# Gate and up product of a hybrid decoder block: where the second half's norm matmuls stand, and which engine does its last squares and low parts

## The chip, the cores and the metric

The kernel runs on one core of one Trainium2 chip. The metric is the device time of one execution in microseconds (us). Three runs of the kernel before gave 1517.66, 1513.57 and 1512.15 us; the median is 1513.57 us.

## What is computed

One decoder block over 1024 tokens of width 1024 in float32: two attention branches (sparse attention and a gated delta rule), an output projection with a residual, then a gated feed-forward network with an inner width of 2816, and a final norm. The change lies where the output projection ends and the feed-forward network begins:

```
x = x + jnp.concatenate([o_nsa, o_gdn], axis=-1) @ w_out
h = rmsnorm(x, norm2_g)
x = x + (jax.nn.silu(h @ w_gate) * (h @ w_up)) @ w_down

def rmsnorm(x, g):
    y = x * lax.rsqrt(jnp.mean(x * x, axis=-1, keepdims=True) + RMS_EPS)
    return y * g
```

## The kernel before

The kernel holds activations with the width on the 128 partitions and the tokens along the free axis, in two halves of 512 tokens (hf 0 and 1) and 8 slices of 128 of the width (dt 0 to 7). To keep float32 accuracy each matmul operand is split in a high part (a rounded copy, written by ScalarE) and a low part (the source less the high part, written by VectorE or GpSimd), and each product of two such pairs is three matmuls: `split3`, lines 116 to 121, high by high (L119), high by low (L120), low by high (L121).

**Output projection.** `woa(hf, dt)` multiplies for one slice; `woa_out(hf, dt)` (L1169 to L1176) adds the residual on VectorE (L1172), stores the result and passes it to `sumsq` (L1185): ScalarE squares it (L1187, tile wx), and for dt 1 to 5 GpSimd adds the square to the running sum sqa (L1191). The squares of dt 6 and 7 are not added: they go as two more tiles to the list parts[hf].

**Norm.** `rnorm_sum` (L1202) sums over partitions on TensorE: for each of four token blocks and each of the three tiles (sqa and the two of parts) a matmul with two columns of ones (L1208). The profile shows two records for each such float32 matmul, so 24. VectorE scales the sum (L1211), GpSimd takes the power of minus one half (L1212), and `rnorm_out` (L1215) spreads the result over the partitions with four matmuls (L1219, 8 records). `normed` (L1356, L1357) scales one slice on VectorE with the result straight from PSUM. `bsplit` (L1360) splits a scaled slice: high part on ScalarE (L1361), low part on the engine that is passed in (L1362).

**Gate and up.** The weights come in blocks b = 0 to 21 (gate and up alternate for 11 pairs of blocks). Every block but the first is made with a scheme of seven products in place of eight, on sums and differences of quarters: of the activations B11, B21 (first half of the tokens), B12, B22 (second half) and the sums T1 to T4, and of the weights A11, A12, A22 and the sums S1 to S4. `Weights.second` (L1335) loads the raw quarters (L1324, five raw buffers), forms the sums on VectorE (L1339 to L1342) and splits them (ScalarE L1199, GpSimd L1200). The sums of block 1 are split behind the power of the second half's norm on GpSimd (mark["pow"], L1343).

Block 0 is done plainly with `prod2` (L1382): 8 steps of k, 24 matmuls, into one bank. The order in the text is: c11 = prod2 with A11, A12 on the first half; `rnorm_sum` of the second half; c21 = prod2 with A21, A22; `rnorm_out`; then the products A11 by B11 and A12 by B21 of blocks 1 and 2 (L1398, 48 matmuls), which need only the first half. Then the second half is scaled and split: 8 times `normed` with `bsplit` on GpSimd (L1410 to L1415), then the differences for T1 to T4 and their splits on VectorE (L1416 to L1427: 16 differences and sums, 16 low parts). With B12 and B22 the two other plain products of block 0 follow (L1437, L1438, 48 matmuls), then for block 1 the products S2 by T2, S3 by T3, S1 by T1, A22 by T4 and S4 by B22, 60 matmuls.

**What sets the order.** Each engine runs its own instructions in order. A planner fixes that order: it takes the instructions in the order of the text, but an instruction that is not ready by its own estimate lets later ones of the same engine pass. `after(ins, prev)` adds an order without a semaphore: ins stands behind prev on their engine. The ring (L1195) is a set of 20 buffers of 128 by 512 that holds the 16 slices of the two halves, the four t2, and later the gate's results (`gated`, L1431), each of which takes the buffer of a slice that is no longer needed. The PSUM pool of this stage has 8 banks.

Of the kernel before, what the change touches and what calls it, by code (L numbers as in the profile page):

```python
# [10 lines left out]
F32 = mybir.dt.float32  # L11
# [8 lines left out]
P = 128  # L20
# [3 lines left out]
KD = D // P  # L24
# [55 lines left out]
def hybrid_block(ctx, tc, xT, xN, pos, cst_d, vec_d, w_tok, w_gdn, cw1, cw2, cpos, w_out, w_gu, w_dn, out):  # L80
# [7 lines left out]
    def mk(pool, shape, tag, dtype=F32, bufs=1):  # L88
        return pool.tile(list(shape), dtype, name=nm(tag), tag=tag, bufs=bufs)
# [10 lines left out]
    def bc(ap, shape):  # L100
        return ap.to_broadcast(list(shape))

    def flat(ap):
        return ap.rearrange("p h t -> p (h t)")
# [4 lines left out]
    mm = nc.tensor.matmul  # L109
# [3 lines left out]
    V = nc.vector  # L113
    G = nc.gpsimd

    def split3(ps, lhs, rhs, first, last, grow=False):

        (lh, ll), (rh, rl) = lhs, rhs
        mm(ps, lhsT=lh, rhs=rh, start=first, stop=False, skip_group_check=grow)  # L119
        mm(ps, lhsT=lh, rhs=rl, start=False, stop=False, skip_group_check=grow)  # L120
        return mm(ps, lhsT=ll, rhs=rh, start=False, stop=last, skip_group_check=grow)  # L121

    def after(ins, prev):

        if prev is not None:
            tc.add_manual_dep(ins.ins, prev.ins.name, mybir.DependencyInfo(
                mybir.DependencyClass.NoSync, mybir.DependencyReason.DATA), reason="order")
        return ins
# [45 lines left out]
    ident = C("ident")  # L174
# [994 lines left out]
    def woa_out(hf, dt):  # L1169
        ps, xt, _ = woas[hf, dt]  # L1170
        x2 = xs2[hf, dt] = ring()
        V.tensor_tensor(out=x2, in0=xt, in1=ps, op=ALU.add)  # L1172
        dma(x3D[hf, dt], x2)
        t = sumsq(sqa[hf], x2, dt, 512, G if dt < 6 else None, flat(mk(pmx, [P, 4, P], "wx", F32, 3)))
        if dt >= 6:
            parts[hf].append(t)  # L1176

    woas = {}
# [6 lines left out]
    def sumsq(sqa, x2, dt, w, eng, tmp):  # L1185
        s_ = tmp if dt else sqa
        act(out=s_[:, :w], in_=x2, func=AF.Square)  # L1187
        if eng is None:
            return tmp
        if dt:  # L1190
            eng.tensor_tensor(out=sqa[:, :w], in0=sqa[:, :w], in1=s_[:, :w], op=ALU.add)  # L1191

    mark = {}
# [8 lines left out]
    def rnorm_sum(parts, w, prev=None):  # L1202

        n = w // P
        ps = bank2("n")
        for j in range(n):
            for q_, t in enumerate(parts):
                after(mm(ps[:, 2 * j:2 * j + 2], lhsT=t[:, j * P:(j + 1) * P], rhs=ones[:, 0:2], start=q_ == 0,  # L1208
                         stop=q_ == len(parts) - 1), prev)
        ms = mk(pc, [P, 2, 4], "ms4", F32, 2)  # L1210
        V.tensor_scalar(ms[:, 0, 0:n], ps[:, 0:2 * n:2], 1.0 / D, EPS, op0=ALU.mult, op1=ALU.add)  # L1211
        mark["pow"] = G.tensor_tensor(out=ms[:, 1, 0:n], in0=ms[:, 0, 0:n], in1=C("mhalf")[:, 0:n], op=ALU.pow)  # L1212
        return ms

    def rnorm_out(ms, w, prev=None):  # L1215

        ps = bank2("n")
        for j in range(w // P):
            after(mm(ps[:, j * P:(j + 1) * P], lhsT=bc(ms[:, 1, j:j + 1], [P, P]), rhs=ident, start=True, stop=True),  # L1219
                  prev)  # L1220
        return ps[:, 0:w]

    merge((scores(us[0]), wa(0)))
# [46 lines left out]
    def bank2(tag="mm"):  # L1270
        return mk(pps2, [P, 512], "mm", F32, 8)
# [84 lines left out]
    def normed(hf, dt, rB):  # L1356
        V.scalar_tensor_tensor(out=xs2[hf, dt], in0=xs2[hf, dt], scalar=VC("g2")[:, dt:dt + 1], in1=rB,  # L1357
                               op0=ALU.mult, op1=ALU.mult)

    def bsplit(B, k, src, eng):  # L1360
        act(out=B[:, 0, k], in_=src, func=AF.Copy)  # L1361
        eng.tensor_tensor(out=B[:, 1, k], in0=src, in1=f32(B[:, 0, k]), op=ALU.subtract)  # L1362
# [16 lines left out]
            wts[b] = Weights(b // 2, b % 2)  # L1379
            wts[b].first() if b else wts[b].plain()  # L1380
    P12 = {}
    def prod2(A, B, A_, B_):  # L1382

        ps = bank2()
        for k in range(8):
            a_, b_ = (A, B) if k < 4 else (A_, B_)
            e = split3(ps, (a_[:, 0, k % 4], a_[:, 1, k % 4]), (b_[:, 0, k % 4], b_[:, 1, k % 4]), k == 0, k == 7)
            if k == 3:
                mid = e
        return ps, mid, e  # L1390


    W = wts.pop(0)
    c11, mid, _ = prod2(W.A11, B11, W.A12, B21)
    ms1_ = rnorm_sum([sqa[1]] + parts[1], 512, mid)
    c21, mid, _ = prod2(W.A21, B11, W.A22, B21)
    rB1 = rnorm_out(ms1_, 512, mid)
    for b in range(1, NAHEAD):  # L1398
        p1, e = prod(wts[b].A11, B11)
        p2, e = prod(wts[b].A12, B21)  # L1400
# [6 lines left out]
    h = [(xs2[0, k], xs2[0, 4 + k], xs2[1, k], xs2[1, 4 + k]) for k in range(4)]  # L1407
    t2 = {}
    B12 = mk(pms, [P, 2, 4, 512], "mns", F32R, 1)
    for k, (h0a, h0b, h1a, h1b) in enumerate(h):  # L1410
        normed(1, k, rB1)
        bsplit(B12, k, h1a, G)
    for k, (h0a, h0b, h1a, h1b) in enumerate(h):
        normed(1, 4 + k, rB1)
        bsplit(B22, k, h1b, G)  # L1415
    for k, (h0a, h0b, h1a, h1b) in enumerate(h):  # L1416
        V.tensor_tensor(out=h0a, in0=h1a, in1=h0a, op=ALU.subtract)
        t2[k] = ring()
# [12 lines left out]
    def gated(o, ps):  # L1431
        half[o] = ring()
        act(out=half[o], in_=ps, func=AF.Silu)

    gated((0, 0), c11)
    gated((1, 0), c21)
    gated((0, 1), prod2(W.A11, B12, W.A12, B22)[0])  # L1437
    gated((1, 1), prod2(W.A21, B12, W.A22, B22)[0])  # L1438

    for p in range(NF // 2):  # L1440
        for j in range(2):
# [287 lines left out]
```

## Time and profile before

| | |
|---|---|
| median of three runs | 1513.57 us |
| the profiled execution, device time | 1515.43 us |
| its span, first to last instruction | 1513.7 us |
| TensorE busy in the span | 95% |
| VectorE, ScalarE, GpSimd busy | 64%, 48%, 48% |
| mean granted TensorE clock | 0.98 |

The profile is of one execution. The span leaves out 1.73 us of the execution's own time. Times in rows are us from the span's start. PE is TensorE's matmul, PEld its weight load, DVE is VectorE, ACT is ScalarE, POOL is GpSimd, SP is the engine that issues the DMAs; a trailing q is an engine's sequencer. PEclk is the granted clock of TensorE as a share of full speed: 1.00 is 2.4 GHz and 0.50 is 1.2 GHz, and a stretch between the two holds both. Matmuls overlap, so the distance from start to start tells what one costs. A bracket at the end of a row gives the idle time ahead of it and what ended it.

### The profile page before, as it was taken

Reading aid. Unit: us, or ns where it says so; the run is one execution under the profiler, and the core shown is the slowest. Engines: PE = TensorE matmul, PEld = TensorE weight load, DVE = VectorE, ACT = ScalarE, POOL = GpSimd, SP = SyncE. Lnnn points to the kernel's source line nnn. Section 1 sums busy time; section 2 is a strip of 40 time slices with the busy share of each in tenths; the row PEclk is TensorE's granted clock in tenths of the full one; section 3 lists DMA queues with packets and bytes.
Section 4 is the critical chain, followed back from the end, with each engine's and each line's share of the span. In section 5 each row is a group of like instructions: output and inputs, shape, how many; then the busy total and the mean of one; then the engine's idle time right before and its main releaser. Section 6 shows DMA issues by size and latency. Waiting matters only on the chain.

```text
span 1513.7 us, 23493 instructions
## 1 busy us (share of the span) xinstructions
PE 1436.1 (95%) x8000; PEld 1225.8 (81%) x8000; DVE 964.8 (64%) x2276; ACT 722.9 (48%) x1604; POOL 727.1 (48%) x763
## 2 busy tenths in 40 slices
PE   8889999989899999999999899999999999999997
PEld 7878877889898787878887688888888887888886
DVE  4326688836635798998956565444444444999955
ACT  5433356236544898788765433323333332344423
POOL 1232235520240665554467666666566663345445
PEclk9999999999998999999999899999999999999998
DMA  8822255487535223101037122222222227544003
GB/s 259 285 65 84 90 184 159 112 189 229 172 108 195 92 74 101 50 22 43 30 124 245 32 88 84 84 84 84 84 84 84 84 84 262 195 135 133 1 1 111
DMA packets 142743, 174.96 MB, mean 116 GB/s; under 512 B 26912, under 2 KB 79392, under 8 KB 142496
## 3 DMA queue, kind: packets, MB, share of 16 engines
q1 hardware_dynamic: 142624, 173.47, 36.6%
q8 instruction: 63, 1.03, 0.3%
q14 instruction: 56, 0.46, 0.1%
HBM read 122.01 MB, written 51.41 MB: 115 GB/s over the span
## 4 chain that ended last, share of the span: by engine, by line
PE 61%; DVE 11%; ACT 5%; issue 4%; POOL 3%; DMA 3%; POOLq 0%; SPq 0%; ACTq 0%; DVEq 0%
PE mm L119 16%; PE mm L121 16%; PE mm L120 16%; PE c L1043 3%; PE b L1063 2%; DVE PT L1066 2%; PE a L610 1%; ACT Ps L1014 1%; DVE cy L429 1%; DMA vT<-gD 1%; PE a L997 1%; PE a L617 1%; ACT PT L1065 1%; DVE tmp L574 1%; PE b L625 1%
## 5 line engine op out<-in xcount | busy, mean ns | idle before, releaser
L1200 POOL TENSOR_TENSOR A<-wq,A 128x512 fp32r<-128x512 f32 x94 | 135.2, 1440 | 87.5 <-ACT A L1199 79.1
L1199 ACT ACTIVATE A<-wq 128x512 fp32r<-128x512 f32 x96 | 60.1, 630 | 133.0 <-PE mm L121 116.9
L119 PE MATMUL mm<-w,xh 128*128 128x256 f32 x384 | 111.7, 291 | 11.7 <-ACT kst L827 6.2
L1066 DVE TENSOR_TENSOR PT<-b,PT 128x512 fp32r<-128x512 f32 (+2 forms) x168 | 103.8, 621 | 19.0 <-ACT PT L1065 17.2
L120 PE MATMUL mm<-w,xh 128*128 128x256 f32 x384 | 110.9, 289 | 1.0 <-POOL w L208 1.0
L121 PE MATMUL mm<-w,xl 128*128 128x256 f32 x384 | 110.6, 288 | 0.0
L1065 ACT ACTIVATE PT<-b 128x512 fp32r<-128x512 f32 (+2 forms) x168 | 89.1, 539 | 37.6 <-PE b L1063 31.2
L1200 POOL TENSOR_TENSOR wk<-wq,wk 128x512 fp32r<-128x512 f32 x61 | 81.5, 1338 | 52.9 <-ACT wk L1199 44.3
L1043 PE MATMUL c<-PT,vs 128*128 128x256 f32 x528 | 92.9, 300 | 0.1
L208 POOL TENSOR_TENSOR w<-wraw,w 128x512 fp32r<-128x512 f32 x48 | 63.4, 1337 | 56.8 <-ACT w L205 56.8
L119 PEld LDWEIGHTS mm<-w,xh 128*128 128x128 f32 x384 | 75.0, 195 | 12.4 <-ACT kst L827 6.4
L1199 ACT ACTIVATE wk<-wq 128x512 fp32r<-128x512 f32 x63 | 39.6, 630 | 87.6 <-PE mm L121 79.9
L119 PE MATMUL mm<-T,A 128*128 128x512 f32 x200 | 79.1, 396 | 0.0
L120 PE MATMUL mm<-T,A 128*128 128x512 f32 x200 | 79.1, 396 | 0.0
L121 PE MATMUL mm<-T,A 128*128 128x512 f32 x200 | 79.1, 396 | 0.0
L120 PEld LDWEIGHTS mm<-w,xh 128*128 128x128 f32 x384 | 75.0, 195 | 1.2 <-POOL w L208 1.2
L119 PE MATMUL mm<-xh,w 128*128 128x512 f32 x192 | 75.6, 394 | 0.0
L121 PE MATMUL mm<-xh,w 128*128 128x512 f32 x192 | 75.2, 392 | 0.0
L121 PEld LDWEIGHTS mm<-w,xl 128*128 128x128 f32 x384 | 74.9, 195 | 0.1
L1043 PEld LDWEIGHTS c<-PT,vs 128*128 128x128 f32 x528 | 73.0, 191 | 2.5 <-DVE PT L1066 0.3
L1501 DVE TENSOR_TENSOR B<-B,mm 128x512 f32<-128x512 f32 x100 | 63.4, 677 | 17.9 <-PE mm L121 15.0
L120 PE MATMUL mm<-xl,w 128*128 128x512 f32 x192 | 74.8, 389 | 0.0
(471 smaller groups left out, 4533.0 us busy)
## 6 DMA issues: line engine op xcount, KB each, us to landing
wq<-in_w_gu SPq DMA_DIRECT2D x92, 256.0 KB, 2.7
aD<-ring SPq DMA_DIRECT2D x44, 256.0 KB, 2.2
ring<-aD SPq DMA_DIRECT2D x44, 256.0 KB, 3.9
raw<-in_w_dn SPq DMA_DIRECT2D x36, 256.0 KB, 3.8
qk<-gD SPq DMA_DIRECT2D x16, 512.0 KB, 4.8
wraw<-in_w_out SPq DMA_DIRECT2D x28, 256.0 KB, 2.9
wraw<-in_w_tok SPq DMA_DIRECT2D x24, 256.0 KB, 3.1
wraw<-in_w_gdn SPq DMA_DIRECT2D x24, 256.0 KB, 2.8
```

The lines of the kernel that those rows point to most:

```text
L119: mm(ps, lhsT=lh, rhs=rh, start=first, stop=False, skip_group_check=grow)
L120: mm(ps, lhsT=lh, rhs=rl, start=False, stop=False, skip_group_check=grow)
L121: return mm(ps, lhsT=ll, rhs=rh, start=False, stop=last, skip_group_check=grow)
L208: (lo or G).tensor_tensor(out=wt[:, 1, k0:k0 + n, :], in0=raw, in1=f32(wt[:, 0, k0:k0 + n, :]), op=ALU.subtract)
L429: V.scalar_tensor_tensor(out=y, in0=cr[:, j:j + 512], scalar=cw[:, j:j + 1], in1=y, op0=ALU.mult, op1=ALU.add)
L1043: mm(po[:, 0:256], lhsT=v, rhs=PT[0:K, a, b_ * 256:(b_ + 1) * 256], start=(n_ == 0 and a == 0), stop=(last and b_ == len(vs) - 1 and a == 1))
L1063: tpose(pt[:, o_:o_ + P], src[:, hh, b * P:(b + 1) * P], ident)
L1065: act(out=PT[0:K, 0, 0:w], in_=pt[0:K, 0:w], func=AF.Copy)
L1066: V.tensor_tensor(out=PT[0:K, 1, 0:w], in0=pt[0:K, 0:w], in1=f32(PT[0:K, 0, 0:w]), op=ALU.subtract)
L1199: act(out=dst[:, 0], in_=src, func=AF.Copy)
L1200: after(eng.tensor_tensor(out=dst[:, 1], in0=src, in1=f32(dst[:, 0]), op=ALU.subtract), prev)
L1501: V.tensor_tensor(out=out_, in0=a_, in1=b_, op=op)
```

## The change

The squares of dt 6 and 7 of the second half are added to sqa on VectorE, so its norm sums one tile in place of three. `prod2` takes a table of functions to call between its steps: in c11, `rnorm_sum` of the second half stands behind step k = 2 and `rnorm_out` behind step k = 6, and the first matmul of the step that follows stands behind the last norm matmul (`split3` has a new argument for it). The second half's scaling and splitting is one loop over d = 0 to 7, and the low parts of B12 and B22 are written by VectorE.

```diff
-    def split3(ps, lhs, rhs, first, last, grow=False):
+    def split3(ps, lhs, rhs, first, last, grow=False, prev=None):
...
-        mm(ps, lhsT=lh, rhs=rh, start=first, stop=False, skip_group_check=grow)
+        after(mm(ps, lhsT=lh, rhs=rh, start=first, stop=False, skip_group_check=grow), prev)
...
-        t = sumsq(sqa[hf], x2, dt, 512, G if dt < 6 else None, flat(mk(pmx, [P, 4, P], "wx", F32, 3)))
-        if dt >= 6:
+        t = sumsq(sqa[hf], x2, dt, 512, G if dt < 6 else V if hf else None, flat(mk(pmx, [P, 4, P], "wx", F32, 3)))
+        if dt >= 6 and not hf:
             parts[hf].append(t)
...
-    def prod2(A, B, A_, B_):
+    def prod2(A, B, A_, B_, between=()):
 
         ps = bank2()
+        prev = None
         for k in range(8):
             a_, b_ = (A, B) if k < 4 else (A_, B_)
-            e = split3(ps, (a_[:, 0, k % 4], a_[:, 1, k % 4]), (b_[:, 0, k % 4], b_[:, 1, k % 4]), k == 0, k == 7)
-            if k == 3:
-                mid = e
-        return ps, mid, e
+            e = split3(ps, (a_[:, 0, k % 4], a_[:, 1, k % 4]), (b_[:, 0, k % 4], b_[:, 1, k % 4]), k == 0, k == 7,
+                       prev=prev)
+            prev = None
+            if k in between:
+                between[k](e)
+                prev = mark["pe"]
+        return ps
...
-    c11, mid, _ = prod2(W.A11, B11, W.A12, B21)
-    ms1_ = rnorm_sum([sqa[1]] + parts[1], 512, mid)
-    c21, mid, _ = prod2(W.A21, B11, W.A22, B21)
-    rB1 = rnorm_out(ms1_, 512, mid)
+    norm1 = {}
+
+    def norm1_sum(e):
+        norm1["ms"] = rnorm_sum([sqa[1]], 512, e)
+
+    def norm1_out(e):
+        norm1["rB"] = rnorm_out(norm1["ms"], 512, e)
+
+    c11 = prod2(W.A11, B11, W.A12, B21, {2: norm1_sum, 6: norm1_out})
+    c21 = prod2(W.A21, B11, W.A22, B21)
+    rB1 = norm1["rB"]
...
-    for k, (h0a, h0b, h1a, h1b) in enumerate(h):
-        normed(1, k, rB1)
-        bsplit(B12, k, h1a, G)
-    for k, (h0a, h0b, h1a, h1b) in enumerate(h):
-        normed(1, 4 + k, rB1)
-        bsplit(B22, k, h1b, G)
+    for d in range(KD):
+        normed(1, d, rB1)
+        bsplit((B12, B22)[d // 4], d % 4, xs2[1, d], V)
```

`rnorm_sum` and `rnorm_out` also store their last matmul in mark["pe"], from which `prod2` takes it.

## Rows read from the trace of the kernel before

**Rows 1.** Part 1 of the page: busy time, share of the span and instructions of each engine.

```profile
PE 1436.1 (95%) x8000; PEld 1225.8 (81%) x8000; DVE 964.8 (64%) x2276; ACT 722.9 (48%) x1604; POOL 727.1 (48%) x763
```

**Rows 2.** The waits of TensorE's matmuls from 870 us to the end: engine, line, what it waited for, us in total, times, longest.

```profile
PE mm L120 <- POOL wk L1200: 2.4, 1, 2.4
```

**Rows 3.** The chain that ended last, in order of time, of the stretch 760 to 920 us: start, us, what.

```profile
835.27 2.58 PE mm L1208 x24
...
845.01 0.90 PE mm L1219 x8
...
847.43 3.82 POOL mns L1362 x3
...
852.62 9.38 issue
...
863.27 3.71 POOL B L1362 x3
...
868.66 1.68 POOL B L1362
```

**Rows 4.** TensorE's timeline: start, us, line, operands, shape.

```profile
829.64 0.39 PE L119 MATMUL mm<-B,A 128*128 128x512 f32 x1
...
831.70 0.39 PE L119 MATMUL mm<-B,A 128*128 128x512 f32 x1
...
858.70 0.39 PE L119 MATMUL mm<-mns,A 128*128 128x512 f32 x1
863.32 0.80 PE L120 MATMUL mm<-mns,A 128*128 128x512 f32 x1 [4.24 <-POOL mns L1362]
...
870.39 0.51 PE L120 MATMUL mm<-B,wk 128*128 128x512 f32 x1 [1.58 <-POOL B L1362]
...
876.53 0.40 PE L119 MATMUL mm<-T,wk 128*128 128x512 f32 x1
```

**Rows 5.** Busy time by stretch: the stretch, its length, then busy us (and instructions) of PE, PEld, DVE, ACT and POOL, the granted clock, the DMA engines' share and GB/s.

```profile
838.70:842.10 3.40, 3.40 (x10) 2.64 (x9) 0.00 (x0) 0.00 (x0) 2.92 (x3) 0.52 0.19 36
...
862.60:869.40 6.80, 5.49 (x12) 3.57 (x12) 3.72 (x3) 2.12 (x4) 6.80 (x6) 0.51 0.14 39
...
829.64:876.53 46.89, 41.08 (x177) 33.02 (x176) 30.47 (x44) 19.40 (x34) 28.10 (x14) 0.89 0.12 36
```

**Rows 6.** GpSimd's timeline.

```profile
838.13 1.02 POOL L1212 TENSOR_TENSOR ms<-ms,cst 128x4 f32<-128x4 f32 x1 [8.50 <-DVE ms L1211]
...
851.21 10.84 POOL L1200 TENSOR_TENSOR A<-wq,A 128x512 fp32r<-128x512 f32 x1
```

**Rows 7.** VectorE's timeline. From 851.21 to the row at 860.24 it runs sixteen instructions on two SBUF sources with no idle time between them.

```profile
829.64 1.28 DVE L1362 TENSOR_TENSOR B<-ring,B 128x512 fp32r<-128x512 f32 x2
830.85 0.68 DVE L1339 TENSOR_TENSOR wq<-wq,wq 128x512 f32<-128x512 f32 x1
831.45 0.67 DVE L1172 TENSOR_TENSOR ring<-xt,mm 128x512 f32<-128x512 f32 x1
...
845.94 5.35 DVE L1357 SCALAR_TENSOR_TENSOR ring<-ring,vec,mm 128x512 f32<-128x512 f32 x8 [7.89 <-PE mm L1219]
851.21 1.28 DVE L1417 TENSOR_TENSOR ring<-ring,ring 128x512 f32<-128x512 f32 x2
...
860.24 0.68 DVE L1362 TENSOR_TENSOR T<-ring,T 128x512 fp32r<-128x512 f32 x1
```

**Rows 8.** ScalarE's timeline.

```profile
832.22 0.64 ACT L1187 ACTIVATE wx<-ring 128x512 f32<-128x512 f32 x1 [1.77 <-DVE ring L1172]
...
864.53 0.60 ACT L1433 ACTIVATE ring<-mm 128x512 f32<-128x512 f32 x1 [5.25 <-POOL B L1362]
```

**Rows 9.** TensorE's timeline earlier in the kernel, in the attention stage: L119 and L120 are of the same step of `split3`, L949 is of another piece of work.

```profile
618.78 0.48 PE L119 MATMUL mm<-mgt,wo 128*128 128x512 f32 x1
619.30 0.73 PE L949 MATMUL a<-ksw,QS 128*128 128x512 f32 x2
619.87 0.40 PE L120 MATMUL mm<-mgt,wo 128*128 128x512 f32 x1
```

**Rows 10.** Busy time by stretch (columns as in rows 5) around three idle times of TensorE elsewhere in the kernel, and of a stretch with 24 records of a norm's sum (809.50).

```profile
809.50:812.50 3.00, 3.00 (x27) 2.92 (x26) 0.85 (x2) 1.26 (x2) 3.00 (x3) 1.00 1.02 366
812.50:816.00 3.50, 3.50 (x21) 2.99 (x20) 0.69 (x1) 1.26 (x2) 3.50 (x4) 1.00 0.79 299
...
597.60:600.00 2.40, 0.06 (x2) 0.02 (x1) 1.57 (x7) 2.33 (x8) 1.97 (x3) 0.98 0.86 322
600.00:603.40 3.40, 3.40 (x10) 2.57 (x10) 1.57 (x6) 1.25 (x4) 0.04 (x1) 0.52 0.29 85
632.00:634.00 2.00, 0.76 (x5) 0.38 (x3) 1.97 (x10) 0.52 (x1) 1.79 (x3) 1.00 0.00 0
1276.00:1279.00 3.00, 0.64 (x4) 0.49 (x3) 1.25 (x1) 0.99 (x2) 2.60 (x3) 1.00 0.99 351
1279.00:1282.40 3.40, 3.40 (x10) 2.62 (x9) 1.42 (x1) 1.83 (x4) 3.40 (x3) 0.52 0.98 336
```

**Rows 11.** Groups of VectorE's instructions by line in the stretch 845.9 to 882.1 us: busy us, mean ns of one, idle time before and its releaser.

```profile
L1362 DVE TENSOR_TENSOR T<-ring,T 128x512 fp32r<-128x512 f32 x16 | 14.8, 958 | 4.8 <-ACT T L1361 4.8
...
L1422 DVE TENSOR_TENSOR ring<-ring,ring 128x512 f32<-128x512 f32 x4 | 3.8, 947 | 0.0
```

**Rows 12.** The DMA issues by line in the stretch 790 to 905 us: KB each and median us from issue to landing.

```profile
wq<-in_w_gu SPq DMA_DIRECT2D x24, 256.0 KB, 3.1
```

More of the change, by code (lines that the diff above doesn't have):

```diff
@@ L1207, in rnorm_sum @@
             for q_, t in enumerate(parts):
-                after(mm(ps[:, 2 * j:2 * j + 2], lhsT=t[:, j * P:(j + 1) * P], rhs=ones[:, 0:2], start=q_ == 0,
-                         stop=q_ == len(parts) - 1), prev)
+                mark["pe"] = after(mm(ps[:, 2 * j:2 * j + 2], lhsT=t[:, j * P:(j + 1) * P], rhs=ones[:, 0:2],
+                                      start=q_ == 0, stop=q_ == len(parts) - 1), prev)
         ms = mk(pc, [P, 2, 4], "ms4", F32, 2)
@@ L1218, in rnorm_out @@
         for j in range(w // P):
-            after(mm(ps[:, j * P:(j + 1) * P], lhsT=bc(ms[:, 1, j:j + 1], [P, P]), rhs=ident, start=True, stop=True),
-                  prev)
+            mark["pe"] = after(mm(ps[:, j * P:(j + 1) * P], lhsT=bc(ms[:, 1, j:j + 1], [P, P]), rhs=ident, start=True,
+                                  stop=True), prev)
         return ps[:, 0:w]
@@ L1436, in hybrid_block @@
     gated((1, 0), c21)
-    gated((0, 1), prod2(W.A11, B12, W.A12, B22)[0])
-    gated((1, 1), prod2(W.A21, B12, W.A22, B22)[0])
+    gated((0, 1), prod2(W.A11, B12, W.A12, B22))
+    gated((1, 1), prod2(W.A21, B12, W.A22, B22))
     for p in range(NF // 2):
```

## The prediction, made before the change was run

> **What bounds the kernel now.** I began with the page's busy shares: TensorE is busy 95% of the span and the next engine 64% [rows 1], so a stage gains only what TensorE stops losing in it. Then the chain of waits, where it meets the change. It runs on matmuls up to 835, takes in a norm sum (24 records, 2.58 us) and a norm output (0.90 us), leaves TensorE, and until 870 consists of the second half's scaling, ScalarE's copy and GpSimd's low parts, with a hole called "issue" of 9.38 us among them [rows 3]. TensorE's own timeline gives the price: it waits 4.24 us for B12's last low part and 1.58 us for B22's [rows 4], and at those two places it runs at half clock: PEclk is 0.52 and 0.51 in 838.7 to 842.1 and in 862.6 to 869.4, which is 1.2 GHz instead of 2.4 [rows 5].
>
> Why do the low parts come so late? Norm output ends near 845.9, and VectorE scales all eight slices in 5.35 us [rows 7]. GpSimd writes three low parts of B12, then starts one of A at 851.21 that takes 10.84 us [rows 6]. In that time VectorE runs sixteen instructions with two SBUF sources back to back, 851.21 to 860.92 [rows 7]; GpSimd's instruction ends 1.1 us after the last of them. So GpSimd was held off all that while; the fourth low part of B12 and all of B22 stood behind it. ScalarE then waited 5.25 us for a ring buffer that GpSimd still read [rows 8], and VectorE 4.8 us for ScalarE [rows 11].
>
> The stage is thus 829.64 (first matmul of c11) to 876.53 (first use of T2): 46.89 us [rows 4, 5]. Its work is fixed: 24 + 24 + 48 + 48 = 144 matmuls by the code. From 829.64 to 831.70 nine cost 2.06 us, 0.229 each [rows 4]: 33.0 us. After 870 TensorE waits for anything over a microsecond in a product just once more, 2.4 us in the next phase [rows 2], so time won here should last to the end.
>
> **The change, part by part.**
>
> *One tile in the norm sum instead of three.* 24 records in 2.58 us become 8: 0.86 us, 1.7 us off TensorE's path. The two additions go to VectorE: two instructions at the 0.60 us pitch of the sixteen, 1.2 us in a queue that is full here [rows 7]. They are not free, as the norm now waits for the second of them.
>
> *Norm sum behind k = 2, output behind k = 6.* In before, both stood behind whole products and found their data ready. The most that the stage can gain is what full speed leaves: 33.0 + 0.86 + 0.90 for norm output [rows 3] = 34.7, so 12.2 us, if neither the norm nor any B or T makes TensorE wait.
>
> When can the norm sum start? TensorE gets past k = 2 at 831.70. The last slice of the output projection is evacuated by VectorE at 831.45 to 832.12, because VectorE is still at first-half low parts until 830.85 and takes a weight sum next; ScalarE squares it from 832.22 to 832.86 [rows 7, 8]. The new addition for dt 6 enters that queue too, ahead of the dt 7 evacuation or in the weight sum's place. So the square stands at 832.9 to 833.5, the addition behind it, perhaps after one 0.68 us weight sum, ends at 833.5 to 834.8. TensorE would wait 1.8 to 3.1 us if nothing passed. Something may pass: the planner lets later work of an engine go by what is not ready, on TensorE too, as where two score matmuls stand between L119 and L120 of one step [rows 9]; here c21's matmuls are ready. But it fills the gap that it expects, not VectorE's real lateness. I take 0.1 to 1.3 us filled (none to six matmuls), so a wait of 0.5 to 3.0 us, and choose 1.8. What is queued behind: all of c11 from k = 3, on TensorE; nobody else.
>
> *What the wait does to the clock.* Two idle times of TensorE of 2.34 and 2.36 us were each followed by 3.4 us at PEclk 0.52; one of 1.24 us had none in its stretch [rows 10]. 24 thin norm records were followed by half clock once (838.7, rows 5) and once not (809.5 and 812.5, rows 10). 1.8 us of wait with 0.86 us of thin records behind it is nearer to the first kind: one stretch of 3.4 us at half clock, costing 1.7 us. Ends: 0 and 3.4.
>
> *The way to the output.* The sum ended at 837.85 [rows 3] and GpSimd's 1.02 us power, behind VectorE's scaling, at 839.15 [rows 6]: 1.3 us. From k = 3 to 6 there are 12 matmuls, 2.7 us: hidden, with 1.4 us to spare. Norm output then ends about 834.2 + 0.9 + 2.7 + 0.9 = 838.7, against 845.9: scaling starts 7.2 us earlier.
>
> *Low parts of B12 and B22 on VectorE, each behind its scaling.* Eight instructions leave GpSimd (the first three took 3.82 us there, rows 3), eight of 0.60 us join VectorE. Scaling costs 0.66 us a slice [rows 7], so from 838.9 the sixteen instructions need 8 x (0.66 + 0.60) = 10.1 us: B22 is complete at about 849. TensorE wants B12 at 829.64 + 96 x 0.229 + 1.8 = 853.4 at full speed and B22 after that. Both waits go, and the half clock around them. What is late next is the T chain: 32 instructions of 0.60 us, 849 to 868.2. T2 is done after 12 of them (856.2, wanted at 864.3), T3 and T1 after 24 (863.4, wanted at 867.1 and 869.9), T4 at 868.2 (wanted at 872.6). It hides, by 4.4 us or more, and by 3.5 us more with the loss above.
>
> Forecast: 12.2 - 1.8 - 1.7 = 8.7 us gained. On the profiled execution (1515.43 us, 1513.7 of it span) that is 1506.7; the median of the runs is 1.86 lower, so 1504.9.
>
> **The rivals.**
>
> *A. The planner fills the wait.* If c21's matmuls stand in the gap, 0 to 1 us is lost and no half clock follows: 11.2 to 12.2 us gained, 1501.4 to 1502.4. For it: TensorE's order shows such passing [rows 9]. Against it: VectorE's lag here is a thing of the run, and the two steps, 2.06 us of matmuls against square, addition and evacuation of 0.64 + 0.60 + 0.67 = 1.9 us, look nearly equal on paper, so a planner sees little to fill.
>
> *B. GpSimd is held off longer.* VectorE now has up to 32 instructions with two SBUF sources in a row in place of sixteen, and three of block 1's low parts (S1, A22, S4) fall into them, since their buffers come free only as blocks 1 and 2 use up A11 and A12. Held until 868.2 they end at 869.5 to 872, and A22 is wanted at 872.6. Only then does its raw buffer reload, 3.1 us to landing [rows 12], then three sums of 0.60, ScalarE's 0.64 [rows 8] and GpSimd's 1.3: block 2's S2 is ready at 877.5, wanted at 864.3 + 60 x 0.233 = 878.3. That just holds. If some of VectorE's instructions are drawn out too, as T's sixteen were (mean 958 ns instead of 0.68 us, so 4.4 us in all, rows 11), it is 3 to 4 us late, with another half-clock stretch of 1.7: 3.2 to 6 us gained, 1507.5 to 1510.4. The Trainium skill, SBUF — State Buffer, section "Who interferes with whom", speaks against the change in this way: a VectorE instruction with two SBUF inputs contends with a GpSimd instruction that reads SBUF, and whoever comes second is blocked. The trace agrees on the contention, with 10.84 us for GpSimd's instruction; it differs in the length, sixteen instructions and not one. By that rule the low parts would end early among the new, shorter runs and B would not happen; by the row it can.
>
> *C. Slower than before: each of VectorE's two-source instructions waits for a GpSimd instruction.* Place: the low parts and the T chain, 40 instructions. Price: about 1.1 us each (L1422's four average 947 ns [rows 11] where 0.68 us is usual [rows 7], together 1.1 us more: one that was held). With 4.4 us of slack and 12.2 us of gain it decides from 15 drawn-out instructions on; with 25 the time is 1513.6 + 25 x 1.1 - 16.6 = 1524.5. Against it: GpSimd has only some five low parts to do in that stretch.
>
> *D. The change doesn't do what it says.* The norm sum could be so late (past 835.1, where it stood before) that the wait and the clock take back more: with 5 us of wait and 3.4 us of clock loss 3.8 us are gained, 1509.8.
>
> **How the numbers follow.** Forecast 0.50, with its own range 1503.0 to 1506.8 (wait 0.5 to 3.0 us, with or without the slow stretch); A 0.22; B 0.18; D 0.05; C 0.05. Predicted 1504.9. The range runs from A's end 1501.3 to B's end 1510.4, leaving out C and little more. What a measurement of this kernel can tell from no change is about 0.5%, 7.6 us: the border is 1506.0. Most of the forecast (0.42), all of A and a little of B lie below it: faster 0.66. The rest of the forecast, B, D and part of C: same 0.30. Slower 0.04.
>
> **What would show it.** Right: 8 norm records after nine (or up to fifteen) matmuls from c11's start; an idle time ahead of them put down to VectorE's addition, one half-clock stretch behind; scaling on VectorE 7 us earlier relative to c11's start; no wait of TensorE for B12, B22 or T; c11's start to T2's first matmul 38 us instead of 46.9. Wrong: a wait of TensorE for a low part of A, S or T from GpSimd (B); VectorE's means above 1 us (C); the norm sum over 5 us behind c11's start (D); or a gain here that a later phase takes back.

## The result, and the profile after

In the first comparison 20 executions of the changed kernel gave a median of 1506.08 us (1498.54 to 1513.05) and 20 of the kernel before 1515.57 us: ratio 0.9941, 95% interval 0.9928 to 0.9954. In a second comparison 12 gave 1509.89 us against 1514.61 us: 0.9969, interval 0.9951 to 0.9987. So the change makes the kernel faster, by 5 to 9 us (0.3 to 0.6%). In the one profiled execution of each comparison gate and up takes the same time to 0.1 us, so what the two differ by most likely lies outside it (see the end of the section on the prediction).

The profiled execution of the changed kernel took 1513.05 us (span 1511.3), the longest of the 20. It reaches the first matmul of c11 at 833.43 us, 3.8 us later than the kernel before did, so times are compared from that matmul on.

Busy times, part 1 of the page (after): GpSimd's count falls by 8, VectorE's rises by 10 [rows 1].

```profile
PE 1436.4 (95%) x7984; PEld 1227.4 (81%) x7984; DVE 967.9 (64%) x2286; ACT 723.6 (48%) x1604; POOL 712.6 (47%) x755
```

The chain that ended last (after): start, us, what. It stays on VectorE from 828 us to the norm, with 0.44 us of "issue", through the first half's scaling and low parts, the last evacuations (VectorE reads a finished product out of its PSUM bank, here L1172), the two new additions and two weight sums. The chain then goes back to TensorE and no longer runs through the second half's scaling and GpSimd, as in [rows 3].

```profile
827.96 1.78 DVE B L1362
829.74 0.66 DVE ring L1357
830.40 0.60 DVE ring L1172
831.14 0.44 issue
831.58 0.68 DVE B L1362
832.26 0.66 DVE ring L1357
832.92 0.60 DVE ring L1172
833.51 0.79 DVE B L1362 x2
834.65 0.67 DVE sqa L1191
835.32 0.60 DVE ring L1172
835.92 0.61 DVE wq L1339
836.56 0.69 DVE wq L1340
837.25 0.61 DVE sqa L1191
837.90 1.35 PE mm L1208 x8
```

TensorE's timeline (after; columns as in [rows 4]).

```profile
833.43 0.39 PE L119 MATMUL mm<-B,A 128*128 128x512 f32 x1
...
835.27 0.39 PE L121 MATMUL mm<-B,A 128*128 128x512 f32 x1
837.90 1.35 PE L1208 MATMUL mm<-ones,sqa 128*128 128x2 f32 x8 [2.25 <-DVE sqa L1191]
839.11 0.77 PE L119 MATMUL mm<-B,A 128*128 128x512 f32 x1
839.68 0.63 PE L120 MATMUL mm<-B,A 128*128 128x512 f32 x1
...
843.26 1.06 PE L1219 MATMUL mm<-cst,ms 128*128 128x128 f32 x8
844.08 0.47 PE L119 MATMUL mm<-B,wk 128*128 128x512 f32 x1
...
872.27 0.40 PE L119 MATMUL mm<-T,wk 128*128 128x512 f32 x1
```

Nine matmuls, then 2.25 us idle for VectorE's second addition, eight norm records, matmuls at half clock, the output after step k = 6. The first use of T2 comes 872.27 - 833.43 = 38.84 us after c11's start, against 46.89 before [rows 4]: 8.05 us won. The same stretch by windows (after; columns as in [rows 5]):

```profile
833.43:872.27 38.84, 36.59 (x161) 30.01 (x160) 33.66 (x52) 19.25 (x32) 8.63 (x6) 0.96 0.14 43
835.70:837.90 2.20, 0.00 (x0) 0.00 (x0) 2.17 (x5) 1.25 (x2) 0.00 (x0) 1.00 0.32 119
837.90:841.30 3.40, 3.40 (x13) 3.01 (x14) 1.31 (x3) 0.64 (x2) 1.77 (x2) 0.59 0.00 0
...
844.70:872.27 27.57, 27.57 (x122) 22.64 (x121) 27.57 (x41) 16.56 (x27) 4.72 (x3) 1.00 0.10 28
```

From 844.70 on TensorE is never idle and the granted clock is 1.00; the two waits and the two half-clock stretches of before [rows 4, 5] have become one of each. Of the waits of matmuls into mm from 872 us to the end (after) only the one of [rows 2] is over half a microsecond, as before:

```profile
PE mm L120 <- POOL wk L1200: 2.5, 1, 2.5
```

GpSimd's timeline (after) no longer has an instruction of 10.84 us [rows 6]:

```profile
839.53 1.40 POOL L1212 TENSOR_TENSOR ms<-ms,cst 128x4 f32<-128x4 f32 x1 [6.11 <-DVE ms L1211]
...
853.95 1.73 POOL L1200 TENSOR_TENSOR A<-wq,A 128x512 fp32r<-128x512 f32 x1 [10.52 <-DVE ring L1425]
856.67 1.30 POOL L1200 TENSOR_TENSOR A<-wq,A 128x512 fp32r<-128x512 f32 x1 [0.99 <-ACT A L1199]
861.60 1.69 POOL L1200 TENSOR_TENSOR wk<-wq,wk 128x512 fp32r<-128x512 f32 x1 [3.62 <-ACT wk L1199]
```

And VectorE's (after): scaling starts at 844.36, the chain of sums and low parts for T ends at 877.69, and only then come block 2's weight sums (L1339).

```profile
844.36 2.06 DVE L1357 SCALAR_TENSOR_TENSOR ring<-ring,vec,mm 128x512 f32<-128x512 f32 x3 [4.31 <-PE mm L1219]
...
853.85 2.38 DVE L1362 TENSOR_TENSOR B<-ring,B 128x512 fp32r<-128x512 f32 x2
...
877.01 0.68 DVE L1362 TENSOR_TENSOR T<-ring,T 128x512 fp32r<-128x512 f32 x1
877.61 0.67 DVE L1339 TENSOR_TENSOR wq<-wq,wq 128x512 f32<-128x512 f32 x1
```

### The profile page after: what moved, and what is told of

Same layout as the page of the kernel before. It is cut to its first block, busy times and chain, and to the rows that moved or that the text cites. A ratio compares the mean times of both kernels' runs of the same rounds, so it can differ in the third digit from the quotient of the medians.

```text
span 1511.3 us, 23459 instructions
## 1 busy us (share of the span) xinstructions
PE 1436.4 (95%) x7984; PEld 1227.4 (81%) x7984; DVE 967.9 (64%) x2286; ACT 723.6 (48%) x1604; POOL 712.6 (47%) x755
## 4 chain that ended last, share of the span: by engine, by line
PE 61%; DVE 12%; ACT 5%; DMA 4%; issue 3%; POOL 2%; SPq 0%; DVEq 0%; ACTq 0%; POOLq 0%
PE mm L119 16%; PE mm L121 16%; PE mm L120 16%; PE c L1043 2%; DVE PT L1066 2%; PE b L1063 2%; ACT Ps L1014 2%; PE a L610 1%; DMA vT<-gD 1%; PE a L617 1%; DVE cy L429 1%; DVE tmp L574 1%; PE a L997 1%; ACT PT L1065 1%; DVE xi L576 1%
## 5 line engine op out<-in xcount | busy, mean ns | idle before, releaser
L1200 POOL TENSOR_TENSOR A<-wq,A 128x512 fp32r<-128x512 f32 x94 | 126.6, 1349 | 97.4 <-ACT A L1199 77.6
L119 PE MATMUL mm<-w,xh 128*128 128x256 f32 x384 | 111.8, 291 | 10.9 <-ACT kst L827 6.2
L120 PE MATMUL mm<-w,xh 128*128 128x256 f32 x384 | 111.0, 289 | 1.0 <-POOL w L208 1.0
L121 PE MATMUL mm<-w,xl 128*128 128x256 f32 x384 | 110.7, 288 | 0.0
L1200 POOL TENSOR_TENSOR wk<-wq,wk 128x512 fp32r<-128x512 f32 x61 | 82.5, 1353 | 55.5 <-ACT wk L1199 46.9
L119 PEld LDWEIGHTS mm<-w,xh 128*128 128x128 f32 x384 | 75.1, 195 | 11.6 <-ACT kst L827 6.4
L119 PE MATMUL mm<-T,A 128*128 128x512 f32 x200 | 79.1, 396 | 0.0
L120 PE MATMUL mm<-T,A 128*128 128x512 f32 x200 | 79.1, 396 | 0.0
L121 PE MATMUL mm<-T,A 128*128 128x512 f32 x200 | 79.1, 396 | 0.0
L1477 POOL TENSOR_TENSOR ring<-ring,ring 128x512 f32<-128x512 f32 x44 | 58.2, 1323 | 39.0 <-DVE ring L1462 26.5
L120 PEld LDWEIGHTS mm<-w,xh 128*128 128x128 f32 x384 | 75.2, 196 | 1.2 <-POOL w L208 1.2
L119 PE MATMUL mm<-xh,w 128*128 128x512 f32 x192 | 75.6, 394 | 0.0
L1509 DVE TENSOR_TENSOR B<-B,mm 128x512 f32<-128x512 f32 x100 | 63.7, 678 | 18.0 <-PE mm L121 17.6
L121 PE MATMUL mm<-xh,w 128*128 128x512 f32 x192 | 75.2, 392 | 0.0
L121 PEld LDWEIGHTS mm<-w,xl 128*128 128x128 f32 x384 | 75.0, 195 | 0.1
```

Of the source, the lines that this page charges most:

```text
L119: after(mm(ps, lhsT=lh, rhs=rh, start=first, stop=False, skip_group_check=grow), prev)
L1200: after(eng.tensor_tensor(out=dst[:, 1], in0=src, in1=f32(dst[:, 0]), op=ALU.subtract), prev)
L1477: G.tensor_tensor(out=t, in0=half[o], in1=t, op=ALU.mult)
L1509: V.tensor_tensor(out=out_, in0=a_, in1=b_, op=op)
```

## The experiments

The theory at the start: the gain comes from the earlier scaling together with the low parts' move off GpSimd, and the 4.1 us that the stage still loses (wait and half clock around the norm) would be a further gain. The rivals: one part alone brings it all, or a later stage takes back what the stage gains. For every kernel the trace gives four times, from the first matmul of c11 to the first on T2 (end of block 0), to block 2's first product of a T, to block 3's first matmul, and to the last matmul of gate and up. The two kernels that were profiled twice, after and e8, agree in them to 0.1 us.

| kernel | T2 | block 2 | block 3 | last | ratio to before, interval |
|---|---|---|---|---|---|
| before | 46.9 | 60.9 | 74.9 | 444.5 | |
| after, and again (e10) | 38.8 | 52.8 | 66.8 | 436.5 | 0.9941 (0.9928 to 0.9954); 0.9969 (0.9951 to 0.9987) |
| e1 | 36.5 | 52.1 | 72.1 | 441.7 | 0.998 (0.9964 to 0.9996) |
| e2 | 38.8 | 56.4 | 70.4 | 440.1 | 0.9953 (0.9934 to 0.9972) |
| e3 | 34.7 | 48.7 | 67.2 | 436.8 | 0.993 (0.9905 to 0.9954) |
| e4 | 38.9 | 52.9 | 66.9 | 436.6 | 0.9961 (0.9944 to 0.9978) |
| e5 | 34.7 | 48.7 | 65.8 | 435.4 | 0.9932 (0.9908 to 0.9956) |
| e6 | 46.9 | 60.9 | 74.9 | 444.5 | 0.999 (0.9972 to 1.0008) |
| e7 | 38.1 | 52.5 | 71.9 | 441.6 | 0.9993 (0.9968 to 1.0018) |
| e8, and again (e11) | 34.7 | 48.7 | 62.7 | 432.3 | 0.9919 (0.9895 to 0.9943); 0.992 (0.9905 to 0.9935) |
| e9 | 40.3 | 55.3 | 74.8 | 444.4 | one execution: 1511.25 us, median of before beside it 1514.61 |
| e12 | 38.1 | 52.5 | 66.7 | 436.3 | 0.9958 (0.994 to 0.9976) |

From block 2's first product to block 3's first matmul is 14.0 us where nothing waits (60 matmuls, 0.233 us each); after block 3 all kernels need the same 369.6 us. What a kernel keeps of its gain is decided between the columns T2 and block 3.

**e1: the kernel before with only the low parts moved to VectorE.**

```diff
-        bsplit(B12, k, h1a, G)
+        bsplit((B12, B22)[d // 4], d % 4, xs2[1, d], V)
```

> The kernel before with one part of the change: the second half's low parts on VectorE, each behind its scaling; squares and norm matmuls as before. Measure: the stage from c11's first matmul to T2's first, 46.9 us in the profile of before and 38.8 in that of after. Theory H (the loss was GpSimd held off while VectorE ran): both waits of TensorE for low parts (4.24 and 1.58) and the half clock around them go, the half clock behind the 24 norm records may stay; stage 37 to 39 us, 8 to 9 us faster than before. Rival N (what counts is that the second half's scaling starts earlier): B12 and B22 are still late, stage 43 to 46 us, at most 3 us faster.

The stage comes out even shorter than in after, 36.5 us: no wait for the norm, and none for a low part. It also has no half clock behind the 24 norm records (granted clock 1.00 from 845.60 to 849.00), where before, e6, e7, e9 and e12 have a stretch of it behind the same records; e7 and e12 reach T2 at 38.1. Why e1's execution was spared was not looked into, so some 1.6 of its 10.4 us may not be the edit's. But of the 10.4 us, 7.6 are gone by block 3. TensorE's waits of e1, 820 to 1000 us:

```profile
PE mm L121 <- POOL wk L1200: 3.6, 1, 3.6
PE mm L119 <- ACT wk L1199: 1.5, 1, 1.5
```

Both are for split weight sums of block 2: its first matmul, due 36.5 + 14.0 = 50.5 us after c11's start, waits for the high part, the first one that takes the low part (L121) waits for that, with half clock behind (matmuls 0.43 us apart). In before block 2 began at 60.9 us and found them ready. The time was won at one place, and the next thing due, wanted 10 us earlier than before, was late.

**e2: the norm's place and the squares as in after, low parts on GpSimd.**

```diff
-        bsplit((B12, B22)[d // 4], d % 4, xs2[1, d], V)
+        bsplit(B12, k, h1a, G)
```

> The other part alone: squares on VectorE, one tile in the norm sum, norm matmuls inside c11; the low parts of B12 and B22 on GpSimd as before. Theory H: GpSimd is held off again, a wait for a low part of B12 or B22 of 1 to 4 us remains although scaling starts 5 us earlier, and the wait for the last square (2 us) is added; stage 41 to 46 us, 1 to 5 us faster than before. Rival N: the earlier start is enough, no wait for low parts; stage 38 to 39.5 us, as in the whole change.

GpSimd is again held off, and yet no matmul waits for a low part: with scaling 5.4 us earlier there was room for it. The loss comes in block 1. GpSimd's timeline and TensorE's waits of e2 (the first row groups the four low parts of B12, of which the last, from 840.37, took 8.45 us):

```profile
836.58 12.24 POOL L1362 TENSOR_TENSOR mns<-ring,mns 128x512 fp32r<-128x512 f32 x4 [2.70 <-ACT mns L1361]
848.78 6.84 POOL L1362 TENSOR_TENSOR B<-ring,B 128x512 fp32r<-128x512 f32 x4
```

```profile
PE mm L1208 <- DVE sqa L1191: 2.2, 1, 2.2
PE mm L119 <- ACT ring L1444: 1.8, 1, 1.8
```

ScalarE's copy of a result out of its PSUM bank (L1444, tile ring) came late: on ScalarE it stood behind the split of a weight sum that VectorE made late (872.22 us, ScalarE 1.12 us idle for L1342). With half clock behind the wait, block 1 takes 17.6 instead of 14.0 us. So either part alone removes the waits of before for B12 and B22; after is ahead by what follows, not by these waits.

**e3: the norm sum three steps of k later, the output in c21.** This takes both losses out of the stage that after still has.

```diff
-    c11 = prod2(W.A11, B11, W.A12, B21, {2: norm1_sum, 6: norm1_out})
-    c21 = prod2(W.A21, B11, W.A22, B21)
+    c11 = prod2(W.A11, B11, W.A12, B21, {6: norm1_sum})
+    c21 = prod2(W.A21, B11, W.A22, B21, {2: norm1_out})
```

> The whole change with the norm sum behind step k = 6 of c11 and the norm output behind step k = 2 of c21. Theory W (the wait for the last square, 2.25 us, and the half clock behind it are what keeps the stage at 38.8): no idle time ahead of the norm sum, no half clock, stage 34.7 to 35.5 us, 3.3 to 4 us faster than the change and 11.5 to 12.2 faster than before. Rival: the thin norm records bring half clock by themselves as they did once in before; stage 36.3 to 37 us. Rival two: T2 or a low part of the weights is now wanted too early and TensorE waits there; stage 36 to 39 us with a wait that names it.

For the stage the theory of the wait held: 34.7 us, the full-speed sum of the prediction (33.0 + 0.86 + 0.90), 4.1 us better than after, and the granted clock stays at 1.00 behind eight records that have no idle time ahead of them (830.70 to 834.10). For the total it fell: at block 3 e3 is 0.4 us behind after. TensorE's timeline of e3 in block 2:

```profile
874.88 0.40 PE L120 MATMUL mm<-T,wk 128*128 128x512 f32 x1
877.96 0.50 PE L121 MATMUL mm<-T,wk 128*128 128x512 f32 x1 [2.69 <-POOL wk L1200]
...
879.84 0.63 PE L119 MATMUL mm<-T,wk 128*128 128x512 f32 x1
880.27 0.63 PE L120 MATMUL mm<-T,wk 128*128 128x512 f32 x1
```

TensorE came 4.1 us earlier and waited 2.69 us for block 2's first low part (GpSimd, L1200), which by after's own trace comes just in time. GpSimd's timeline and TensorE's of after:

```profile
883.71 1.30 POOL L1200 TENSOR_TENSOR wk<-wq,wk 128x512 fp32r<-128x512 f32 x1
```

```profile
886.74 0.40 PE L121 MATMUL mm<-T,wk 128*128 128x512 f32 x1
```

The low part ends at 885.01, so after has only 1.7 us to spare there. The 4.1 us that it loses at the norm cover a lateness that in e3 costs 18.5 - 14.0 = 4.5 us in block 2, the wait and a stretch at half clock.

**e4: after with the three tiles of before in the norm sum (24 records).**

```diff
-        norm1["ms"] = rnorm_sum([sqa[1]], 512, e)
+        norm1["ms"] = rnorm_sum([sqa[1]] + parts[1], 512, e)
```

> The whole change but with the squares of dt 6 and 7 as two more tiles of the norm sum, as before (24 records instead of 8), so VectorE adds nothing. The norm sum can start when the last square is written, 1.1 us sooner in the profile of after, and lasts 1.7 us longer at full clock. Expected: wait 1.0 to 1.3 us instead of 2.25, stage 38.5 to 40 us, within 1.5 us of the change. If the additions on VectorE were the cause of the wait, it would vanish and the stage be 37 us.

Without the additions the wait shrinks to 0.6 us (1.0 to 1.3 were expected), for ScalarE's last square, and 16 records more take its place: 38.9 against 38.8 us. The squares' move to VectorE neither gains nor loses.

**e5 to e8: the order of VectorE's queue.** Block 2's weights are late because their sums (L1339 to L1342) stand behind the T chain and block 1's evacuations. e5 is e3 with the sums of blocks 1 and 2 named earlier in the text, ahead of the loop of T4; e6 does the same to the kernel before, e7 to e1.

```diff
+    wts[1].second()
+    wts[2].second()
     for k, (h0a, h0b, h1a, h1b) in enumerate(h):
...
-            W.second()
+            if b >= NAHEAD:
+                W.second()
```

> The kernel with the norm sum behind k = 6 and the output behind k = 2 of c21, and with the weights of blocks 1 and 2 prepared ahead of the T4 loop in the text, so that VectorE makes block 2's four weight sums before T4 and not behind its whole chain. Measure: from c11's first matmul to the last of gate and up, 444.5 us in before, 436.5 in the change, 436.8 with the norm sum later alone (which was 4.1 us ahead at T2 and lost it in block 2). Theory V (block 2's weights are late because their sums stand at the end of VectorE's queue): the wait of 2.7 us for a low part of block 2 and the half clock behind it go, 432 to 433.5 us, 11 to 12.5 us faster than before. Rival S (the raw loads or GpSimd's splitting are late by themselves): the wait stays, 436 to 437.5. Rival T (T4 now comes too late): no wait for weights but one for T4 of 1 to 3 us, 434 to 437.

> The kernel before with that last edit alone (block 2's weight sums ahead of T4). In before TensorE waits for nothing in blocks 1 and 2, since the stage ends 8 us later, so theory V expects no change: 443.5 to 445.5 us from c11 to the end of gate and up. If the sums' place were worth something by itself, it would be 441 or less.

> Low parts on VectorE and norm matmuls as in before (that kernel reached T2 10.4 us sooner but lost 7.6 us of it in blocks 1 and 2, 441.7 us to the end of gate and up), now with block 2's weight sums ahead of T4. Theory V: the 6 us lost in block 2 shrink to 0 to 3, the 1.6 us in block 1 stay or grow as T4 comes later: 435.5 to 439 us. Rival S: 441 to 442.

In e5 the wait for weights is gone and another has come, so that it ends at 435.4 us and not at the 432 to 433.5 of theory V. VectorE's timeline of e5:

```profile
869.87 0.70 DVE L1465 TENSOR_TENSOR ring<-ring,mm 128x512 f32<-128x512 f32 x1
878.02 1.10 DVE L1339 TENSOR_TENSOR wq<-wq,wq 128x512 f32<-128x512 f32 x1 [7.46 <-DMA wq<-in_w_gu]
879.04 0.67 DVE L1466 TENSOR_TENSOR ring<-ring,mm 128x512 f32<-128x512 f32 x1
```

```profile
PE mm L119 <- DVE ring L1466: 2.8, 1, 2.8
```

The planner let block 3's first weight sum go ahead of block 1's evacuations; its raw quarter landed late, VectorE stood 7.46 us in front of it, and TensorE waited 2.81 us for a PSUM bank that VectorE had to empty. e7 shows the same (3.5 us for L1455); it ends at 441.6 us, as rival S had it, but by this wait and not by late weights. e6 is the control: where block 2's weights are not late, naming them earlier changes nothing. e8 is e5 with one more edge, block 3's first weight sum behind block 1's last evacuation:

```diff
-            V.tensor_tensor(out=flat(s1), in0=flat(r21), in1=flat(r22), op=ALU.add)
+            after(V.tensor_tensor(out=flat(s1), in0=flat(r21), in1=flat(r22), op=ALU.add),
+                  mark["evac"] if 2 * self.p + self.j == NAHEAD else None)
...
-            V.tensor_tensor(out=u2, in0=u2, in1=prod(W.S4, B22)[0], op=ALU.add)
+            e_ = V.tensor_tensor(out=u2, in0=u2, in1=prod(W.S4, B22)[0], op=ALU.add)
+            if b == 1:
+                mark["evac"] = e_
```

> The last combination (norm sum later, block 2's weight sums ahead of T4) with one more order edge: block 3's first weight sum stands behind the last evacuation of block 1 on VectorE. In the run without it VectorE waited 7.5 us for block 3's raw weights with block 1's evacuations queued behind it, and TensorE waited 2.8 us for a bank. Theory Q (what is left is only that order in VectorE's queue): no wait of TensorE from c11 to block 3, 432 to 433 us from c11 to the end of gate and up (435.4 without the edge, 436.5 in the change), 12 us faster than before. Rival R (the raw weights of block 3 are late, since GpSimd frees their buffers late): TensorE waits for a weight of block 3 instead, 434 to 436 us.

TensorE is busy all through (windows of e8, c11 to T2 and T2 to block 3; columns as in [rows 5]):

```profile
826.09:860.78 34.69, 34.69 (x161) 28.83 (x160) 30.73 (x47) 18.49 (x31) 8.30 (x6) 1.00 0.16 48
860.78:888.78 28.00, 28.00 (x121) 22.54 (x120) 21.55 (x31) 11.89 (x22) 23.32 (x14) 1.00 0.25 77
```

Now the stage's whole 12.2 us last to the end of gate and up (432.3). Twice measured, once beside after on one chip:

> The changed kernel again, beside the next one on one chip: 38.8 us from c11's first matmul to T2's, some 436.5 us to the end of gate and up, ratio to the kernel before 0.993 to 0.996.

> The kernel of e8 again, beside the changed one on one chip. If its gain of 4.2 us in gate and up over the changed kernel (432.3 against 436.5 us from c11's first matmul) is one of the kernel: ratio to the kernel before 0.990 to 0.993, 2 to 5 us below the changed kernel's median. If the 4.2 us were of that one execution: the same time as the changed kernel within 1 us.

1503.12 us (0.992) against 1509.89 us (0.9969) for after. The intervals, 0.9905 to 0.9935 and 0.9951 to 0.9987, don't overlap: e8 beats both kernels. It is 6.8 us below after, more than the 2 to 5 expected; gate and up accounts for 4.1 of them in both profiles of e8.

**e9: gaps in VectorE's run, in the kernel before.** Is GpSimd held because VectorE's two-source instructions follow one another without a break?

```diff
+    gap = mk(pc, [P, 64], "gap")
...
-        V.tensor_tensor(out=h0a, in0=h1a, in1=h0a, op=ALU.subtract)
+        e_ = V.tensor_tensor(out=h0a, in0=h1a, in1=h0a, op=ALU.subtract)
+        after(V.memset(gap, 0.0), e_)
```

(and so for the differences of t2 and the sums of T1)

> The kernel before, with a small memset of 128 by 64 on VectorE behind each of the twelve differences and sums of T2, T3 and T1 (so VectorE's sixteen two-source instructions in a row are broken up; its output is not changed). Theory (GpSimd's low part is held off as long as VectorE's two-source instructions follow one another without a gap, 10.84 us before): the instruction of GpSimd that starts with them ends after 2 to 4 us, B12's and B22's low parts come 6 us or more earlier, TensorE's waits of 4.24 and 1.58 us go or shrink to under 2 us in all, and the first matmul of c11 to the first on T2 takes 38 to 42 us in place of 46.9. Rival (the length does not hang on such gaps, or a memset makes none): GpSimd's instruction takes 11 to 14 us, as VectorE's run is now longer by twelve memsets, and the stretch takes 47 to 50 us.

GpSimd's and VectorE's timelines of e9:

```profile
846.96 1.85 POOL L1200 TENSOR_TENSOR A<-wq,A 128x512 fp32r<-128x512 f32 x1
848.77 1.74 POOL L1362 TENSOR_TENSOR mns<-ring,mns 128x512 fp32r<-128x512 f32 x1
```

```profile
846.96 0.68 DVE L1418 TENSOR_TENSOR ring<-ring,ring 128x512 f32<-128x512 f32 x1
847.61 0.11 DVE L1419 MEMSET gap<- 128x64 f32 x1
847.68 1.67 DVE L1421 TENSOR_TENSOR ring<-ring,ring 128x512 f32<-128x512 f32 x1
```

The low part that took 10.84 us takes 1.85: it ends 1.2 us after the first memset begins. From there the two engines take turns, and VectorE's instruction takes 1.67 us where 0.68 is usual. The stage gains 6.6 us (40.3), with 1.4 us left of the wait for B22. The theory held, and then the kernel gave all of it back: 3.65 us of waiting for block 2's low parts (POOL wk L1200), 0.73 us in two smaller waits, and half clock; 74.8 us at block 3, like before. Of the change's two parts it has neither, and it shows the trap by itself.

**e12: e1 with both mends of e8** (the two diffs above). Is the earlier norm needed at all?

> e1's half of the change (the second half's low parts of B12 and B22 on VectorE; norm matmuls and last squares as before) with both mends of e8: the weight sums of blocks 1 and 2 named ahead of the last sums of T4, and block 3's first weight sum behind block 1's last evacuation. If only VectorE's order stood in the way, e1's 36.5 us to T2 last: 432 to 436 us from c11's first matmul to the end of gate and up, ratio to the kernel before 0.992 to 0.995. If the earlier norm is needed (VectorE's chain of some 33 us then starts 9 us later relative to TensorE than in e8, whose block 2 weights had less slack than that), TensorE waits again in blocks 1 and 2, for low parts of weights or of T: 438 to 442 us, ratio 0.996 to 1.000.

It came out 0.3 us above the first range and well below the second: 436.3 us, and the list of TensorE's waits in 820 to 1010 us is empty. Its ratio, 0.9958, lies between the two forecasts, and its interval reaches into both. What e8 has over it, 4.0 us, is hardly waiting: 3.4 us lie ahead of T2, 1.7 of them for 24 norm records instead of 8 and the rest half clock behind these records (granted clock 0.56 from 841.4 to 844.8); 0.6 us come in blocks 1 and 2. So with VectorE's order mended, the low parts' move alone keeps what the whole change keeps in gate and up. But block 2's first low part comes just in time there: it ends at 885.9 us, and the matmul that takes it starts at 885.94, 0.34 us after the one ahead of it in place of 0.23. So the earlier norm isn't needed to keep what the low parts gain; as e8 has it, it brings 4.0 us more.

## Why the prediction came out as it did

The forecast was 8.7 us, from 1513.57 to 1504.9; the stage gave 8.05 and the medians 9.5 and 4.7. The first median, 1506.08, lies within the forecast's own range and 0.1 us above its border of 1506.0 for a clear gain, the second, 1509.89, near rival B's end of the whole range. So the outcome "faster", given 0.66, holds by the intervals of the ratios and not by that border. Point by point:

- **One tile in the norm sum.** Predicted 0.86 us for eight records, measured 839.11 - 837.90 = 1.21, part of it at half clock. The price was the wait for the additions, and e4 shows that the two are equal.
- **The wait.** Predicted 0.5 to 3.0, taken as 1.8; measured 2.4 from when the tenth matmul could have started (835.27 + 0.23). The mechanism was right to the instruction: dt 7's evacuation began 1.82 us after c11's start, as in before (1.81), with dt 6's addition in the place of a weight sum. Two weight sums, not one, stood ahead of dt 7's addition, and the 0.1 to 1.3 us that I let the planner fill did not come: nine matmuls, then nothing. What sets it is VectorE's queue, busy from 828 us on with the first half's scaling and low parts.
- **Half clock.** Predicted one stretch at 1.7 us; one came (granted clock 0.59 in 837.9 to 841.3). 38.84 - 33.0 - 1.21 - 0.82 (output) - 2.40 leaves 1.4 us for it.
- **Scaling 7.2 us earlier.** It was 5.4: 844.36 - 833.43 = 10.9 us after c11's start, against 16.3 [rows 4, 7]. The way from norm sum to output was worked out at full clock, 2.7 us for 12 matmuls; it took 4.15, as the half clock that the same forecast expects falls on them.
- **Low parts on VectorE.** Predicted 10.1 us for the sixteen instructions and nothing for GpSimd. They ended 856.23 - 844.36 = 11.9 us after scaling began: a difference for T stood among them (0.6), and one instruction was drawn out by 1.1 us beside GpSimd's low part (the rows at 853.85 and 853.95). The T chain has two more such. That is rival C's mechanism three times, where fifteen were needed to decide.
- **T hides with 4.4 us or more, plus 3.5.** It hid, with 2.9 us to spare: T4's last low part ended at 877.69, 44.3 us after c11's start, and was wanted some 47.2 us after it (38.84 + 36 x 0.233).
- **A** (the planner fills) fell. **D** fell: the norm sum stood 4.5 us behind c11's start.
- **B** was right about the place and wrong about the condition. GpSimd was not held in after, so the weights of block 2 came in time, by 1.7 us, where the prediction, with GpSimd held, had 0.8. But no held GpSimd is needed to make them late: in e1 and e3 GpSimd's instructions took 1.3 to 1.75 us each, and block 2 was late because VectorE's queue puts its sums last.
- **"Time won here should last to the end"** is the weak step. It was argued from one row of waits after 870 us [rows 2], which tells what is late at before's pace and not what would be at a faster one. In after it held (8.05 us at T2, 8.0 at the end of gate and up) by 1.7 us of margin; in e1, e3 and e9, which gained 10.4, 12.2 and 6.6 us in the stage, it didn't.

The sum was right, then, partly by luck: the predicted losses (3.5 us; measured 4.1) cost nothing, since without them, as e3 shows, the time would have been the same. What was right by its mechanism is the stage: where the waits come from, that they go, and what the norm costs in their place.

Outside gate and up the profiled execution of after was 3.8 us slower ahead of c11 and 1511.3 - 833.43 - 436.5 = 241.4 us long behind it, against 239.6 of before. In e10, the same kernel, the two were 831.9 and 238.3 us. Over all profiles of this study the stretch ahead of c11 lay between 824.2 and 837.2 us, with no order by kernel. That scatter is why one execution can't tell a gain of 8 us here, and it may be what the two comparisons differ by, which is not shown; what sets it was not looked into.

## What to carry to other kernels

Before you add up a gain from removed waits, ask for each resource that is due soon after, not only in the stage, when it will be ready if the stage ends earlier; a list of waits at the old pace doesn't show it. Where a change gains in its stage and the total stands still (e1 and e9; e3 beside after), look at the next product for a wait that wasn't there, and then at the order of the queue that makes what it waits for. A wait that costs nothing now may be covering for another: remove both or neither.

## What the hardware showed

GpSimd's low part on two SBUF sources was held for as long as VectorE's run of two-source instructions lasted, and ended 1.1 to 1.2 us after the run's end or first break: 10.84 us in before (run to 860.92, end 862.05), 8.45 in e2 (a break of 0.21 us in the run at 847.67, end 848.82), 6.43 in e8 (run to 870.75, end 871.90; e5, e7 and e12 alike), 1.85 in e9 (memset at 847.61, end 848.81). In e8 it costs TensorE nothing: block 2's first low part still ends 0.9 us before it is wanted (874.40 and 875.25). In a run each VectorE instruction starts 0.08 us before the one ahead of it ends (0.60 us apart, 0.68 long). The Trainium skill, SBUF — State Buffer, section "Who interferes with whom", says that the port pair that VectorE and GpSimd share is an exclusive lock and that issue order decides who blocks. These rows agree for single instructions (e9's turns). They add that a run of VectorE without a break held GpSimd off from one instruction to the next, sixteen times in before. Why after's VectorE queue let GpSimd through each time is not shown: it has two-source instructions in a row too, and so has e8's, where GpSimd got through three times and was held once. Most of these low parts stand close behind ScalarE's high parts, which may make the break. That wasn't tried.
